# Two trunk layers on one core: earlier bank readers and splits in the first layer, half products by row blocks, a bank counted free a tick later, GpSimd's sum first

## The chip, the cores and the metric

The kernel runs on one core of one Trainium2 chip. The metric is the device time of one execution in microseconds (us), the median of the runs shown. Smaller is better.

## What is computed

Two post-norm layers over 512 rows of 1024 columns, in float32. Cut to what matters:

```python
def even_layer(x):                                  # layer 0
    q, k, v, g_ret, xb, g_lru = split(x @ w_in)     # each 1024 wide, 8 heads of 128
    ret = group_norm(retention(rope(q), rope(k), v)) * silu(g_ret)
    lru = rg_lru_branch(xb) * silu(g_lru)           # causal conv of width 4, two gate products, scan
    return concat(ret, lru) @ w_out

def odd_layer(x):                                   # layer 1
    q, k, v, g = split(x @ w_in)                    # 16 query/key heads of 128, 8 value heads of 256
    out = (softmax(q1 k1) - lam * softmax(q2 k2)) @ v     # causal, per head
    out = out * rsqrt(mean(out ** 2) + eps) * subln_g * (1 - lambda_init) * silu(g)
    return out @ w_out

for layer in (even_layer, odd_layer):
    x = layer_norm(alpha * x + layer(x))
```

## The kernel before

Every float32 product is three fp32r matmuls (`mm3`, L155): each operand is split into a high part, cast on ScalarE (L152), and a low part, the difference, on VectorE (L153). That holds for the weights as well, which come by DMA as 128x1024 pieces named w0, w1, ... in the order of use. There are five buffers of split weights, so a weight's cast has to wait until TensorE is done with the weight five places earlier (w89 takes the buffer of w84). A piece's DMA, cast and subtraction run ahead of its use as far as these buffers let them.

TensorE's order is written out by hand. The big projections form the backbone; after each of their steps (a *tick*, `side.tick()`) a queue, `Side`, may place one small step of retention, RG-LRU or attention, as soon as the number of ticks that its generator yielded has gone by (`RET_START`, `LRU_GATES`, `ATT_FREE` and the like). SyncE's DMA order is also written by hand. The orders of ScalarE, VectorE and GpSimd come out of a scheduler, by priorities: `tc.high_priority(n)` lifts what stands under it by n. Each engine then runs its list strictly from front to back.

Products leave TensorE in PSUM banks: four for the big ones (`pj`), two for scores and gates (`sc`), one for attention values (`av`) and one for transposes (`tp`). A product that takes a bank again waits for the last reader of what was in it.

Layer 0, RG-LRU (`lru`, one column block c of 128 at a time): ScalarE reads the product xb twice out of its bank, as a copy (L553) and scaled (L555, tile xc); three VectorE steps finish the convolution (L558); xc is split; after `LRU_GATES[c]` ticks TensorE multiplies it by the gate weights (pr, then pi). `silu` (L483, L484) reads the gate projections gl and gr. Retention (`rs`, rsd, r) and the output product out0 (columns of head 0 and 1) stand between these on TensorE.

Layer 1: the query and key projections of one head run while the attention of another is placed between them. For heads 2 to 7 the gate (g) and value (v) projections are not made as two products: `gates_values` (gv1, gv2, gv3) forms them from seven half products over block sums of the operands, prepared beforehand. `product` walks such a half product; its first two, into the banks gv?a0, gv?a1 and gv?b0, gv?b1, use the plain blocks of x. Attention of head hd and row block qb has these steps: scores as, masked maximum (L694), exponential e (L697), weights wt (transposed, split as w12, w13 and so on after the head and the block), values po, then GpSimd's mean of squares ave (L733) and power ars (L395), the normed block o on VectorE (L736), o's transposes back into po's bank, and the split of those into om, the operand of the output product oo. With one `av` bank the next po has to wait until om of the block before has been read.

```python
        if own:
            av[0] = side.now + ATT_FREE
```

This line (L744) tells the queue when the bank may be asked for again; `spare[0]` is true in the stages that make queries and keys.

The last layer norm: the output product of the last heads ends with row blocks 2 and 3. For block 2 (`late`), one half of the columns goes over ScalarE and GpSimd (L419, L420, L424), the other over VectorE; for block 3 both halves go over VectorE (L428, L430). `rsqrt` (L395) is GpSimd's power. Four output DMAs on SyncE close the kernel.

Of the kernel before, what the change touches and what calls it, by code (L numbers as in the profile page):

```python
# [11 lines left out]
ALU = mybir.AluOpType  # L12
# [5 lines left out]
KT = D // P  # L18
SB = S // P
# [8 lines left out]
RET_START = (13, 13, 13, 13, 13, 13, 13, 8)  # L28
RET_SCORES = (4, 4, 4, 7)
RET_NORM = (8, 7, 8, 7, 8, 6, 5, 5)  # L30
LRU_GATES = (12, 12, 13, 12, 12, 12, 9, 12)
LN_TURN = 15
ATT_START, ATT_GAP = (12,) * 7 + (7,), (8,) * 7 + (7,)
ATT_SCORES = (7, 7, 7, 8)
# [3 lines left out]
ATT_FREE, ATT_LENT = 2, 8  # L38

P_ROPE, P_SCORES, P_SQUARE, P_GROUP, P_VALUE = 50, 13, 60, 5, 60  # L40
P_CONV, P_GATES = 9, 5
P_LN, P_LAST, P_WEIGHTS, P_ATT = 10, 10, 450, 337
P_LAST_GROUP = 500
WARM_UP = 8
EARLY = 2

# [57 lines left out]
def trunk(ctx: ExitStack, tc: tile.TileContext, a):  # L104
# [289 lines left out]
    def rsqrt(var, out):  # L394
        nc.gpsimd.tensor_tensor(out=out, in0=var, in1=nhalf[:, :1], op=ALU.pow)  # L395

    def layer_norm(y, sb, gb, late=False, src=None, then=lambda: None):
        hv = [y[:, sb, hf * HALF:hf * HALF + HALF] for hf in range(2)]
        src = [hv[0], src or hv[1]]
        st = stats.pop(sb, None)  # L400
        if st is None:
            st = small.tile([P, 2, 6], F32, tag="bst", name="bst", bufs=2)
            for hf in range(2):
                nc.vector.bn_stats(out=st[:, hf], in_=hv[hf])
        mv = small.tile([P, 2], F32, tag="bmv", name="bmv", bufs=2)
        nc.vector.bn_aggr(out=mv, in_=st)
        rs = small.tile([P, 1], F32, tag="lrs", name="lrs", bufs=2)
        ve = small.tile([P, 1], F32, tag="rs", name="lve")
        nc.vector.tensor_scalar(out=ve, in0=mv[:, 1:2], scalar1=EPS, scalar2=None, op0=ALU.add)  # L409
        rsqrt(ve, rs)  # L410
        then()
        if late:


            nc.vector.scalar_tensor_tensor(out=hv[0], in0=hv[0], scalar=mv[:, 0:1], in1=gb[0][0], op0=ALU.subtract, op1=ALU.mult)
            yield
            nm = small.tile([P, 1], F32, tag="lnm", name="lnm", bufs=1)
            tc.keep_in_program_order(nc.vector.tensor_scalar(out=nm, in0=mv[:, 0:1], scalar1=rs, scalar2=-1.0, op0=ALU.mult, op1=ALU.mult))
            nc.scalar.activation(out=hv[1], in_=hv[1], func=AF.Identity, scale=rs, bias=nm)  # L419
            nc.gpsimd.tensor_tensor(out=hv[1], in0=hv[1], in1=gb[0][1], op=ALU.mult)  # L420
            yield
            tc.keep_in_program_order(nc.vector.scalar_tensor_tensor(out=hv[0], in0=hv[0], scalar=rs, in1=gb[1][0], op0=ALU.mult, op1=ALU.add))
            yield 0, hv[0]
            tc.keep_in_program_order(nc.gpsimd.tensor_tensor(out=hv[1], in0=hv[1], in1=gb[1][1], op=ALU.add))  # L424
            yield 1, hv[1]
            return
        for hf in range(2):
            nc.vector.scalar_tensor_tensor(out=hv[hf], in0=src[hf], scalar=mv[:, 0:1], in1=gb[0][hf], op0=ALU.subtract, op1=ALU.mult)  # L428
        for hf in range(2):
            nc.vector.scalar_tensor_tensor(out=hv[hf], in0=hv[hf], scalar=rs, in1=gb[1][hf], op0=ALU.mult, op1=ALU.add)  # L430
            yield hf, hv[hf]
# [116 lines left out]
            split(n1, cut(m, ALL, h % 2))  # L548

    def lru(c, ps, m):  # L550
        with tc.high_priority(P_CONV):
            xb = temp(f"xbp{c}")
            nc.scalar.copy(out=xb, in_=ps)  # L553
            xc = temp(f"xc{c}")
            nc.scalar.activation(out=xc, in_=ps, func=AF.Identity, scale=conv_w(3, c), bias=conv_b(c))  # L555
            for w in range(3):
                sh = 3 - w
                nc.vector.scalar_tensor_tensor(out=xc[:, sh:], in0=xb[:, :S - sh], scalar=conv_w(w, c), in1=xc[:, sh:], op0=ALU.mult, op1=ALU.add)  # L558
        with tc.high_priority(P_GATES):
# [12 lines left out]
        nc.scalar.activation(out=i, in_=pi, func=AF.Sigmoid, bias=gbx(c))  # L572

        nc.scalar.activation(out=t, in_=t, func=AF.Tanh, scale=sp4[:, c:c + 1])
        nc.vector.tensor_tensor(out=i, in0=i, in1=xc, op=ALU.mult)  # L575
        d = xc
        r = temp(f"r{c}")

        nc.scalar.activation(out=r, in_=t, func=AF.Ln, bias=1.0)
        nc.scalar.activation(out=r, in_=r, func=AF.Exp, scale=-1.0)  # L580
        nc.vector.scalar_tensor_tensor(out=d, in0=t, scalar=1.0, in1=r, op0=ALU.add, op1=ALU.mult)
        nc.vector.scalar_tensor_tensor(out=d, in0=d, scalar=2.0, in1=r, op0=ALU.subtract, op1=ALU.mult)  # L582
        nc.scalar.activation(out=r, in_=t, func=AF.Sqrt)  # L583
# [26 lines left out]
    for kind, i in ev:  # L610
        if kind == "v":
            if i:
                for j in range(4):
                    side.need(job["ret", j], lambda: j in seen)
            v = v_even(i)
        elif kind == "xb":
            if i % 2 == 0:
                raw = load(f"gw{i}", [P, 4 * P], a["gw"][i // 2], pl=es, tag="es")
                gw[0] = pair(two, [P, 4 * P], "gw", f"gw{i}", bufs=1)
                split(raw, gw[0])  # L620
            job["lru", i] = side.add(lru(i, t_unit(x, f"xb{i}"), mixes(("lru", i // 2))), "lru", 2)
        elif kind == "q":
            dec[i] = load(f"dec{i}", [P, S], a["dec"][i], pl=two, tag="dec")
            q[i] = rope(t_unit(x, f"q{i}"), "q", f"q{i}")
        elif kind == "k":
            job["ret", i] = side.add(retention(i, q.pop(i), rope(t_unit(x, f"k{i}"), "k", f"k{i}"), v, dec.pop(i), mixes(("ret", i // 2))), "ret", 1, RET_START[i])
        elif kind in ("ro", "lo", "out"):
            even_out({"ro": ("ret",), "lo": ("lru",), "out": ("lru", "ret")}[kind], i, f"{kind}{i}")
        else:
            ps = t_unit(x, f"{kind}{i}")  # L630
            if len(users) >= 5:
                side.need(job[users[-5]])
            users.append(("ret" if kind == "gr" else "lru", i))
            g = gp.tile([P, S], F32, tag="g", name=f"{kind}{i}")
            silu(ps, g, f"{kind}{i}")
            gates[kind, i] = g
        if (kind, i) == ("gr", 1):
            for sb in range(SB):
                nc.sync.dma_start(out=y[:, sb], in_=a["x"][sb])
# [44 lines left out]
    def attention(hd, qb, q, k, m):  # L684
# [57 lines left out]
            split(pm.rearrange("p (i s) -> p i s", s=P), cut(m, ALL, ALL, slice(qb * P, qb * P + P)))  # L742

        if own:  # L744
            av[0] = side.now + ATT_FREE

    oj, om, vs, vt, av = {}, {}, {}, {}, [0]

# [67 lines left out]
    def gates_values(i):  # L816
# [3 lines left out]
        def total(k):  # L820
            return lambda kt, n: tuple(sx[:, k, x, kt, n * P:n * P + P] for x in range(2))

        def product(ps, left, start, then=lambda: None):
            for j in range(2):
                if j:
                    then()
# [24 lines left out]
        one = [bank(ps_pj, "pj", f"gv{i}a{n}") for n in range(2)]  # L851
        two = [bank(ps_pj, "pj", f"gv{i}b{n}") for n in range(2)]
        p1, u, p7, low = [], [], [], []
        product(one, block(0, 0), True)
        copies(one, "p1", p1)
        product(two, block(0, 1), True)
        gate(two, p1, 0)
        product(one, total(0), False)
        copies(one, "u", u)
# [19 lines left out]

    def odd_end(sb):  # L880
        nonlocal rest
        last = sb == SB - 1
        norm = layer_norm(y, sb, gb1, sb == SB - 2, residual.get(1) if last else None, (lambda: rest()) if last else (lambda: None))

        def steps():
            for t in norm:
                if t is not None:
                    nc.sync.dma_start(out=a["out"][sb, :, t[0] * HALF:t[0] * HALF + HALF], in_=t[1])
                if sb == SB - 2:
                    yield  # L890

        if sb == SB - 2:
            it = steps()
            next(it)
            rest = lambda: next(it, None)
        else:
            for _ in steps():
                pass

    def past(g):  # L900
        if g >= 0:
# [160 lines left out]
```

## Time and profile before

| | |
|---|---|
| median of 3 runs | 919.15 us (918.99 to 919.6) |
| profiled execution | 919.45 us |
| its span | 917.7 us |
| TensorE busy | 905.8 us, 99% of the span |
| VectorE busy | 718.1 us, 78% |
| ScalarE busy | 517.6 us, 56% |
| GpSimd busy | 113.1 us, 12% |

The span is what the profiler saw between the first and the last instruction; the profiled execution's own time is 1.75 us longer. The engines are PE (TensorE), DVE (VectorE), ACT (ScalarE), POOL (GpSimd) and SP (SyncE). A row of a timeline gives an instruction's start in the span, how long it took, its line, what it wrote and read, and, in brackets, how long its engine was idle before it and whom it waited for. The end of a matmul is modelled, so the rows of TensorE overlap.

### The profile page before, as it was taken

What the parts mean: (1) busy time and instruction counts of PE and PEld (TensorE: products, weight loads), DVE (VectorE), ACT (ScalarE), POOL (GpSimd) and SP (SyncE); (2) the same over time, 40 slices, a digit from 0 to 9 for tenths busy, and PEclk for the clock granted to TensorE, in tenths of its full rate; (3) what the DMA queues carried; (4) which work ended last, traced back from release to release, by engine and by line L of the source; (5) the groups of instructions that cost most, each with busy time, mean ns of one, the idle gap of its engine ahead of it and who ended that gap; (6) DMA issues with size and microseconds to landing.
All of it is one profiled execution on the core that took longest, in us unless ns stands there. A gap on an engine that the chain in (4) does not pass through costs nothing.

```text
span 917.7 us, 11876 instructions
## 1 busy us (share of the span) xinstructions
PE 905.8 (99%) x4258; PEld 750.6 (82%) x4258; DVE 718.1 (78%) x1191; ACT 517.6 (56%) x846; POOL 113.1 (12%) x190
## 2 busy tenths in 40 slices
PE   9999999999999999999999999999999999999996
PEld 7888887888888888888888878888888888888885
DVE  5887977958868998897868887748877668867687
ACT  5567787546575668533456666435655355665440
POOL 2311010110102010010101120000120100201112
PEclk9999999999999999999999999999999999999999
DMA  8985463872829471434842226646247382178102
GB/s 288 283 278 149 125 186 91 245 203 58 263 78 270 113 205 51 169 129 149 326 179 70 69 70 229 229 161 252 70 136 250 142 321 92 58 265 276 45 1 92
DMA packets 46524, 152.93 MB, mean 167 GB/s; under 512 B 6145, under 2 KB 6273, under 8 KB 45697
## 3 DMA queue, kind: packets, MB, share of 16 engines
q1 hardware_dynamic: 41472, 135.39, 41.5%
q0 software_dynamic: 4992, 16.78, 9.5%
q8 instruction: 33, 0.54, 0.2%
q14 instruction: 27, 0.21, 0.1%
HBM read 139.57 MB, written 37.75 MB: 193 GB/s over the span
## 4 chain that ended last, share of the span: by engine, by line
PE 87%; DVE 6%; ACT 3%; issue 2%; POOL 1%; DMA 1%; SPq 0%; DVEq 0%; ACTq 0%; POOLq 0%
PE oo_ps L157 8%; PE gr_ps L157 5%; PE out_ps L157 4%; PE q_ps L157 4%; PE gl_ps L157 4%; PE ev_ps L157 4%; PE k_ps L157 4%; PE xb_ps L157 4%; PE po L157 3%; PE as L157 3%; PE ov_ps L157 2%; PE gv3a L157 2%; PE gv2a L157 2%; PE eo_ps L157 2%; PE og_ps L157 2%; PE gv3b L157 2%
## 5 line engine op out<-in xcount | busy, mean ns | idle before, releaser
L697 ACT ACTIVATE e<-as,nm 128x128 f32<-128x128 f32 (+3 forms) x64 | 33.2, 524 | 33.5 <-DVE nm L694 33.3
L704 POOL TENSOR_SCALAR zr<-z 128x1 f32<-128x1 f32 x32 | 16.4, 511 | 248.1 <-ACT e L697 248.1
L736 DVE SCALAR_TENSOR_TENSOR o<-po,ars,og 128x256 f32<-128x256 f32 x32 | 15.5, 484 | 35.0 <-POOL ars L395 35.0
L186 POOL DMA_DIRECT2D t<-t x24 | 19.2, 799 | 160.3 <-DMA t<-in_od_w 157.7
L733 POOL TENSOR_SCALAR ave<-ss,zr 128x1 f32<-128x1 f32 x32 | 16.4, 512 | 141.2 <-ACT po L730 135.2
L186 POOL DMA_DIRECT2D t<-in_od_w x24 | 19.1, 796 | 117.9 <-DMA t<-in_od_w 117.8
L694 DVE CUSTOM_DVE_ANT_0 as<-as,mask 128x128 f32<-128x128 f32 (+3 forms) x64 | 30.4, 506 | 2.3 <-PE as L157 2.3
L730 ACT ACTIVATE po<-po 128x256 f32<-128x256 f32 x32 | 11.9, 371 | 24.6 <-PE po L157 24.4
L575 DVE TENSOR_TENSOR xbp<-xbp,xc 128x512 f32<-128x512 f32 x8 | 5.5, 692 | 17.5 <-ACT xbp L572 17.5
L395 POOL TENSOR_TENSOR ars<-ave,nhalf 128x1 f32<-128x1 f32 x32 | 18.8, 587 | 2.7
L705 DVE SCALAR_TENSOR_TENSOR e<-e,zr,e 128x128 f32<-128x128 f32 (+3 forms) x32 | 17.6, 549 | 0.8
L558 DVE SCALAR_TENSOR_TENSOR xc<-xbp,vecs,xc 128x509 f32<-128x509 f32 (+2 forms) x24 | 17.8, 744 | 0.2
L395 POOL TENSOR_TENSOR lrs<-lve,nhalf 128x1 f32<-128x1 f32 x8 | 7.3, 912 | 83.1 <-DVE lve L409 83.1
L514 DVE TENSOR_TENSOR rsd<-rs,dec 128x512 f32<-128x512 f32 (+3 forms) x32 | 15.5, 484 | 2.1 <-PE rs L157 1.9
L278 DVE TENSOR_TENSOR y<-oo_ps,y 128x512 f32<-128x512 f32 x23 | 15.3, 685 | 2.2 <-PE oo_ps L157 2.1
L567 ACT ACTIVATE t<-pr,vecs 128x512 f32<-128x512 f32 x8 | 5.5, 688 | 17.5 <-PE pr L157 17.4
L709 PE MATMUL wt<-ident,e 128*128 128x128 f32 x80 | 13.9, 272 | 0.0
L152 ACT CAST hh<-ht 128x512 fp32r<-128x512 f32 x8 | 4.7, 588 | 15.5 <-PE ht L654 15.5
L709 PEld LDWEIGHTS wt<-ident,e 128*128 128x128 f32 x80 | 10.5, 140 | 3.4
L583 ACT ACT_TABLE_LOAD x8 | 10.3, 1283 | 4.2 <-DVE xc L582 4.1
L702 DVE RECIPROCAL zr<-z 128x1 f32<-128x1 f32 x32 | 5.2, 162 | 9.6 <-ACT e L697 9.4
L697 ACT ACTIVATION_READ_ACCUMULATOR e<-as,nm 128x1 f32 x64 | 12.5, 195 | 0.0
(2844 smaller groups left out, 3478.0 us busy)
## 6 DMA issues: line engine op xcount, KB each, us to landing
w_r<-in_od_w SPq DMA_DIRECT2D x58, 512.0 KB, 5.9
w_r<-in_ev_w SPq DMA_DIRECT2D x47, 512.0 KB, 5.1
t<-in_od_w SPq DMA_DIRECT2D x48, 256.0 KB, 5.5
sx<-sd SPq DMA_DIRECT2D x24, 512.0 KB, 5.7
w_r<-t SPq DMA_DIRECT2D x24, 512.0 KB, 3.3
w_r<-in_ev_wo SPq DMA_DIRECT2D x16, 512.0 KB, 4.5
w_r<-in_od_wo SPq DMA_DIRECT2D x16, 512.0 KB, 4.7
t<-in_od_w POOLq DMA_DIRECT2D x24, 256.0 KB, 5.2
```

The source lines that it names most:

```text
L157: nc.tensor.matmul(out=out, lhsT=l[n == 2], rhs=r[n == 1], start=start and n == 0, stop=stop and n == 2, **kw)
L186: nc.gpsimd.dma_start(out=dst, in_=two, max_dma_last_dim=4 * D, accum_op=ALU.add)
L395: nc.gpsimd.tensor_tensor(out=out, in0=var, in1=nhalf[:, :1], op=ALU.pow)
L514: nc.vector.tensor_tensor(out=s[:, :n], in0=ps[:, :n], in1=dec[:, :n], op=ALU.mult)
L558: nc.vector.scalar_tensor_tensor(out=xc[:, sh:], in0=xb[:, :S - sh], scalar=conv_w(w, c), in1=xc[:, sh:], op0=ALU.mult, op1=ALU.add)
L694: nc.vector.tensor_tensor_reduce(out=ps[:, :n], in0=ps[:, :n], in1=mask[:, S - n:], scale=-QK_SCALE, scalar=3.0e38, op0=ALU.add, op1=ALU.m ...
L697: nc.scalar.activation(out=e, in_=ps[:, :n], func=AF.Exp, scale=-1.0, bias=nm, accum_out=z[:, mp:mp + 1])
L704: nc.gpsimd.tensor_scalar(out=zr[:, 1:2], in0=z[:, 0:1], scalar1=z[:, 0:1], scalar2=EPS, op0=ALU.mult, op1=ALU.mult)
L705: nc.vector.scalar_tensor_tensor(out=ee[0], in0=ee[1], scalar=zr[:, 0:1], in1=ee[0], op0=ALU.mult, op1=ALU.add)
L709: nc.tensor.transpose(out=pt[:, kb * P:kb * P + P], in_=ee[0][:, kb * P:kb * P + P], identity=ident)
L733: nc.gpsimd.tensor_scalar(out=ve, in0=ss, scalar1=zr[:, 1:2], scalar2=None, op0=ALU.add)
L736: nc.vector.scalar_tensor_tensor(out=o, in0=po[:, :2 * P], scalar=rs, in1=gates[qb, hd // 2][:, hc:hc + 2 * P], op0=ALU.mult, op1=ALU.mult)
```

## The change

Five parts. In layer 0, the two ScalarE reads of xb's bank for columns 3 and 5, their split, and the silu of the gates gl3 and gl5 get priority 80 (before 9, 5 and 0), as does the split of xc7; the gate products of column 3 come one tick later. In `gates_values` the first two half products go by row blocks: both weights are taken at the start and all four steps of the first row block come ahead of those of the second. Outside the query and key stages the `av` bank is counted free one tick later. In the last layer norm GpSimd's add stands right behind its multiply, and the closures that issued the two are simpler.

```diff
-LRU_GATES = (12, 12, 13, 12, 12, 12, 9, 12)
+LRU_GATES = (12, 12, 13, 13, 12, 12, 9, 12)
...
+P_CONV, P_GATES, P_OUT = 9, 5, 80
+OUT_NEXT = (3, 5)
...
             nc.gpsimd.tensor_tensor(out=hv[1], in0=hv[1], in1=gb[0][1], op=ALU.mult)
+            nc.gpsimd.tensor_tensor(out=hv[1], in0=hv[1], in1=gb[1][1], op=ALU.add)
             yield
             tc.keep_in_program_order(nc.vector.scalar_tensor_tensor(out=hv[0], in0=hv[0], scalar=rs, in1=gb[1][0], op0=ALU.mult, op1=ALU.add))
-            yield 0, hv[0]
-            tc.keep_in_program_order(nc.gpsimd.tensor_tensor(out=hv[1], in0=hv[1], in1=gb[1][1], op=ALU.add))
-            yield 1, hv[1]
+            yield from enumerate(hv)
...
-        with tc.high_priority(P_CONV):
+        with tc.high_priority(P_OUT if c in OUT_NEXT else P_CONV):
             xb = temp(f"xbp{c}")
             nc.scalar.copy(out=xb, in_=ps)
             xc = temp(f"xc{c}")
             nc.scalar.activation(out=xc, in_=ps, func=AF.Identity, scale=conv_w(3, c), bias=conv_b(c))
...
-        with tc.high_priority(P_GATES):
+        with tc.high_priority(P_OUT if c in OUT_NEXT or c == 7 else P_GATES):
             t2 = part(S, f"xc{c}")
             split(xc, t2)
...
-            silu(ps, g, f"{kind}{i}")
+            with tc.high_priority(P_OUT if kind == "gl" and i in OUT_NEXT else 0):
+                silu(ps, g, f"{kind}{i}")
...
-            av[0] = side.now + ATT_FREE
+            av[0] = side.now + ATT_FREE + (not spare[0])
...
+            if apart:
+
+                ws = [take(3) for _ in range(2)]
+                for n in range(2):
+                    for kt in range(KT // 2):
+                        c = kt % 2 * HALF
+                        mm3(ps[n], left(kt, n), cut(ws[kt // 2], ALL, slice(c, c + HALF)), kt == 0, kt == KT // 2 - 1)
+                        side.tick()
+                return
...
-        product(one, block(0, 0), True)
+        product(one, block(0, 0), True, apart=True)
...
-        product(two, block(0, 1), True)
+        product(two, block(0, 1), True, apart=True)
```

Where this moves instructions is shown at three places. In all rows the number after a name counts tiles and has no other meaning; lines of the changed kernel lie one or two away.

ScalarE in layer 0, where out0 of the first head pair runs (xb3_ps is the bank that out0 takes next), before:

```order
L152 CAST w24h_1352<-w24_r_1351 128x1024
L152 CAST retm0h_639<-rq1_1168 128x512
L152 CAST w25h_1572<-w25_r_1571 128x1024
L152 CAST lrum1h_1036<-xc2_1063 128x512
L152 CAST r20h_1330<-rsd20_1328 128x512
L553 COPY xbp3_1379<-xb3_ps_1308 128x512
L555 ACTIVATE xc3_1381<-xb3_ps_1308,vecs_204 128x512
```

And after:

```order
L153 CAST w24h_1352<-w24_r_1351 128x1024
L153 CAST w25h_1572<-w25_r_1571 128x1024
L153 CAST lrum1h_1036<-xc2_1063 128x512
L553 COPY xbp3_1379<-xb3_ps_1308 128x512
L555 ACTIVATE xc3_1381<-xb3_ps_1308,vecs_204 128x512
L153 CAST retm0h_639<-rq1_1168 128x512
L153 CAST r20h_1330<-rsd20_1328 128x512
```

The two reads of xb3's bank, L553 and L555, now stand ahead of the casts of retm0 and r20. On VectorE, gl3 (L484) moves six rows forward in the same stretch, from behind the scan (L587) and rq1's last product (L547) to ahead of rq1's first (L542).

TensorE at the start of gv1, before:

```order
L157 MATMUL gv1a0_4926<-w84h_4751,hh_3481 128x512
L157 MATMUL gv1a0_4926<-w84l_4752,hh_3481 128x512
L157 MATMUL gv1a0_4926<-w84h_4751,hl_3482 128x512
L157 MATMUL gv1a1_4927<-w84h_4751,hh_3481 128x512
L157 MATMUL gv1a1_4927<-w84l_4752,hh_3481 128x512
L157 MATMUL gv1a1_4927<-w84h_4751,hl_3482 128x512
L157 MATMUL gv1a1_4927<-w84h_4751,hh_3481 128x512
L157 MATMUL gv1a1_4927<-w84l_4752,hh_3481 128x512
L157 MATMUL gv1a1_4927<-w84h_4751,hl_3482 128x512
L709 MATMUL wt12_4954<-ident_3479,e102_4872 128x128 x3
L157 MATMUL gv1a0_4926<-w85h_4837,hh_3481 128x512
```

And after:

```order
L158 MATMUL gv1a0_4926<-w84h_4751,hh_3481 128x512
L158 MATMUL gv1a0_4926<-w84l_4752,hh_3481 128x512
L158 MATMUL gv1a0_4926<-w84h_4751,hl_3482 128x512
L158 MATMUL gv1a0_4926<-w85h_4837,hh_3481 128x512
L158 MATMUL gv1a0_4926<-w85l_4838,hh_3481 128x512
L158 MATMUL gv1a0_4926<-w85h_4837,hl_3482 128x512
L158 MATMUL gv1a0_4926<-w85h_4837,hh_3481 128x512
L158 MATMUL gv1a0_4926<-w85l_4838,hh_3481 128x512
L158 MATMUL gv1a0_4926<-w85h_4837,hl_3482 128x512
L711 MATMUL wt12_4960<-ident_3479,e102_4872 128x128 x3
L158 MATMUL gv1a1_4927<-w84h_4751,hh_3481 128x512
```

The second row block (gv1a1) with w84 stood ahead of the first block's w85; now it comes behind it, and w84 is in use until later.

VectorE in gv1, from e103 (attention of head 1, map 0, block 3) to om1l of the block before, before:

```order
L705 SCALAR_TENSOR_TENSOR e103_4978<-e113_4986,zr_4988,e103_4978 128x512
L153 TENSOR_TENSOR w90l_5048<-w90_r_5046,w90h_5047 128x1024
L736 SCALAR_TENSOR_TENSOR o12_5035<-po12_5019,ars_5031,og02_4075 128x256
L153 TENSOR_TENSOR w91l_5108<-w91_r_5106,w91h_5107 128x1024
L694 ISA as200_5056,nm_5060<-as200_5056,mask_4095 128x128
L694 ISA nm_5060 128x1
L694 ISA as210_5064,nm_5068<-as210_5064,mask_4095 128x128
L694 ISA nm_5068 128x1
L847 TENSOR_TENSOR og10_5099<-gv1b0_4928,p110_5006 128x512
L702 RECIPROCAL zr_5072<-z_5055 128x1
L703 TENSOR_SCALAR zr_5072<-zr_5072,z_5055,nlam_3727 128x1
L153 TENSOR_TENSOR w13l_5086<-wt13_5080,w13h_5085 128x512
L705 SCALAR_TENSOR_TENSOR e200_5062<-e210_5070,zr_5072,e200_5062 128x128
L153 TENSOR_TENSOR om1l_4272<-po12_5019,om1h_4271 128x2x128
```

And after:

```order
L707 SCALAR_TENSOR_TENSOR e103_4978<-e113_4986,zr_4988,e103_4978 128x512
L154 TENSOR_TENSOR w89l_5012<-w89_r_5010,w89h_5011 128x1024
L738 SCALAR_TENSOR_TENSOR o12_5041<-po12_5025,ars_5037,og02_4075 128x256
L154 TENSOR_TENSOR w90l_5018<-w90_r_5016,w90h_5017 128x1024
L858 TENSOR_TENSOR og10_5099<-gv1b0_4928,p110_5006 128x512
L696 ISA as200_5056,nm_5060<-as200_5056,mask_4095 128x128
L696 ISA nm_5060 128x1
L696 ISA as210_5064,nm_5068<-as210_5064,mask_4095 128x128
L696 ISA nm_5068 128x1
L816 SCALAR_TENSOR_TENSOR og10_5099<-p110_5006,og10_5099 128x512
L704 RECIPROCAL zr_5072<-z_5055 128x1
L705 TENSOR_SCALAR zr_5072<-zr_5072,z_5055,nlam_3727 128x1
L707 SCALAR_TENSOR_TENSOR e200_5062<-e210_5070,zr_5072,e200_5062 128x128
L154 TENSOR_TENSOR w91l_5108<-w91_r_5106,w91h_5107 128x1024
L154 TENSOR_TENSOR w13l_5086<-wt13_5080,w13h_5085 128x512
L154 TENSOR_TENSOR om1l_4272<-po12_5025,om1h_4271 128x2x128
```

The split of w89, which before stood ten rows further up, comes here; w90l, w91l follow it one place later each, and L814 (L816 after) now stands ahead of om1l. gv2 and gv3 move alike: w115l and w141l come behind the row of e303 and e503, and w117l and w143l right ahead of om3l and om5l.

## Rows read from the trace of the kernel before

**Rows 1.** The page: the span, and busy time with share and instructions.

```profile
span 917.7 us, 11876 instructions
...
PE 905.8 (99%) x4258; PEld 750.6 (82%) x4258; DVE 718.1 (78%) x1191; ACT 517.6 (56%) x846; POOL 113.1 (12%) x190
```

**Rows 2.** Timeline of TensorE: start, duration, instruction, idle before it.

```profile
139.26 0.51 PE L157 MATMUL out_ps<-w21h,lrum0h 128*128 128x512 f32 x1 [0.37 <-DVE gl L484]
...
140.46 0.38 PE L157 MATMUL rs<-q2h,k2h 128*128 128x256 f32 x1 [0.23 <-DVE rsd L514]
...
142.28 0.50 PE L157 MATMUL out_ps<-w21h,lrum0h 128*128 128x512 f32 x1 [0.50 <-ACT xc L555]
...
342.76 0.50 PE L157 MATMUL pr<-xc7l,gw6h 128*128 128x512 f32 x1 [0.41 <-DVE xc7l L153]
...
533.47 0.39 PE L157 MATMUL gv1a<-w84h,hl 128*128 128x512 f32 x1
534.27 0.50 PE L157 MATMUL gv1a<-w84h,hh 128*128 128x512 f32 x1 [0.41 <-DVE om1l L153]
534.61 0.40 PE L157 MATMUL gv1a<-w84l,hh 128*128 128x512 f32 x1
...
543.31 0.51 PE L157 MATMUL gv1b<-w86h,hh 128*128 128x512 f32 x1 [0.20 <-DVE om1l L153]
...
551.35 0.39 PE L157 MATMUL po<-ov00h,w13h 128*128 128x256 f32 x1 [0.22 <-DVE om1l L153]
...
596.44 0.39 PE L157 MATMUL po<-ov10h,w22h 128*128 128x256 f32 x1 [0.16 <-DVE om2l L153]
```

**Rows 3.** Timeline of ScalarE and VectorE in out0 of layer 0.

```profile
134.14 0.60 ACT L483 ACTIVATE gl_sg<-gl_ps 128x512 f32<-128x512 f32 x1
...
138.53 0.68 DVE L484 TENSOR_TENSOR gl<-gl_ps,gl_sg 128x512 f32<-128x512 f32 x1
...
147.79 0.68 DVE L153 TENSOR_TENSOR xc3l<-xc,xc3h 128x512 fp32r<-128x512 f32 x1
```

**Rows 4.** Timeline of VectorE at the gate product of column 7.

```profile
342.03 0.68 DVE L153 TENSOR_TENSOR xc7l<-xc,xc7h 128x512 fp32r<-128x512 f32 x1
```

**Rows 5.** Timeline of VectorE in gv1.

```profile
538.53 1.22 DVE L153 TENSOR_TENSOR w89l<-w_r,w89h 128x1024 fp32r<-128x1024 f32 x1
...
544.64 1.23 DVE L153 TENSOR_TENSOR w90l<-w_r,w90h 128x1024 fp32r<-128x1024 f32 x1 [0.72 <-ACT w90h L152]
...
550.88 0.42 DVE L153 TENSOR_TENSOR om1l<-po,om1h 128x256 fp32r<-128x256 f32 x1
551.21 0.68 DVE L814 SCALAR_TENSOR_TENSOR og<-p,og 128x512 f32<-128x512 f32 x1
```

**Rows 6.** Timeline of GpSimd, VectorE and TensorE in gv2.

```profile
666.70 1.47 POOL L733 TENSOR_SCALAR ave<-ss,zr 128x1 f32<-128x1 f32 x1 [1.06 <-ACT po L730]
...
666.87 1.22 DVE L153 TENSOR_TENSOR w116l<-w_r,w116h 128x1024 fp32r<-128x1024 f32 x1
...
672.21 0.42 DVE L153 TENSOR_TENSOR om3l<-po,om3h 128x256 fp32r<-128x256 f32 x1
...
674.10 0.28 PE L157 MATMUL po<-ov10h,w33h 128*128 128x256 f32 x1
```

**Rows 7.** The page's groups: count, busy time, mean ns, idle before.

```profile
L733 POOL TENSOR_SCALAR ave<-ss,zr 128x1 f32<-128x1 f32 x32 | 16.4, 512 | 141.2 <-ACT po L730 135.2
...
L395 POOL TENSOR_TENSOR ars<-ave,nhalf 128x1 f32<-128x1 f32 x32 | 18.8, 587 | 2.7
```

**Rows 8.** Timeline of GpSimd and VectorE in the last 9 us.

```profile
909.35 1.45 POOL L420 TENSOR_TENSOR y<-y,ln 128x512 f32<-128x512 f32 x1 [1.25 <-ACT y L419]
911.20 0.92 POOL L395 TENSOR_TENSOR lrs<-lve,nhalf 128x1 f32<-128x1 f32 x1 [0.40 <-DVE lve L409]
912.09 1.26 POOL L424 TENSOR_TENSOR y<-y,ln 128x512 f32<-128x512 f32 x1
...
912.29 2.27 DVE L430 SCALAR_TENSOR_TENSOR y<-y,lrs,ln 128x512 f32<-128x512 f32 x2
```

More of the change, by code (lines that the diff above doesn't have):

```diff
@@ L40 @@
 P_ROPE, P_SCORES, P_SQUARE, P_GROUP, P_VALUE = 50, 13, 60, 5, 60
-P_CONV, P_GATES = 9, 5
+P_CONV, P_GATES, P_OUT = 9, 5, 80
 P_LN, P_LAST, P_WEIGHTS, P_ATT = 10, 10, 450, 337
 P_LAST_GROUP = 500
+OUT_NEXT = (3, 5)
 WARM_UP = 8
@@ L395, in rsqrt, with layer_norm @@
         nc.gpsimd.tensor_tensor(out=out, in0=var, in1=nhalf[:, :1], op=ALU.pow)
-    def layer_norm(y, sb, gb, late=False, src=None, then=lambda: None):
+    def layer_norm(y, sb, gb, late=False, src=None):
         hv = [y[:, sb, hf * HALF:hf * HALF + HALF] for hf in range(2)]
@@ L410, in layer_norm @@
         rsqrt(ve, rs)
-        then()
         if late:
@@ L555, in lru @@
             nc.scalar.activation(out=xc, in_=ps, func=AF.Identity, scale=conv_w(3, c), bias=conv_b(c))
+        with tc.high_priority(P_CONV):
             for w in range(3):
@@ L821, in total, with product @@
             return lambda kt, n: tuple(sx[:, k, x, kt, n * P:n * P + P] for x in range(2))
-        def product(ps, left, start, then=lambda: None):
+        def product(ps, left, start, then=lambda: None, apart=False):
+            if apart:
[6 more added lines that the diff above has]
+                return
             for j in range(2):
@@ L881, in odd_end @@
         nonlocal rest
-        last = sb == SB - 1
-        norm = layer_norm(y, sb, gb1, sb == SB - 2, residual.get(1) if last else None, (lambda: rest()) if last else (lambda: None))
+        norm = layer_norm(y, sb, gb1, sb == SB - 2, residual.get(1) if sb == SB - 1 else None)
         def steps():
             for t in norm:
-                if t is not None:
+                if t is None:
+                    yield
+                else:
                     nc.sync.dma_start(out=a["out"][sb, :, t[0] * HALF:t[0] * HALF + HALF], in_=t[1])
[L889 to L898, printed above, removed]
+        it = steps()
+        rest = lambda: next(it, None)
+        rest()
     def past(g):
```

## The prediction

> **What bounds the kernel now.** I read the page first: TensorE is busy 905.8 of 917.7 us [rows 1], and the chain that ended last lies on it almost throughout. So the kernel ends when TensorE has got through its hand-written list, and a change that leaves the list's length alone can win only what TensorE waits, plus the tail behind its last matmul. Next I read the waits of TensorE and looked each up in its timeline [rows 2]. The reader is to see there that idle time of TensorE understates a wait. gv1a at 534.27 shows 0.41 idle; its start lies 0.80 behind the row ahead, where neighbours lie 0.23 apart, and the next row follows after 0.34 instead of 0.23. So that wait costs 0.57 + 0.11 = 0.68: its idle figure plus about 0.28. With this the waits that the change aims at cost: gl in layer 0 0.65, rsd 0.51, xc 0.78, xc7l 0.69, gv1a 0.69, gv1b 0.48, the fourth attention block of head 1 (po at 551.35) 0.50, po at 596.44 0.44 and its twin one pair of heads later the same. That is 5.2 us, the most that can be won ahead of the tail.
>
> **The change, part by part.** Times below are of the profiled execution (919.45; span 917.7, 1.75 around it). I replayed the new order of each engine by hand: every instruction starts when its engine's predecessor and its inputs are done, and takes what the same instruction took in the trace.
>
> *Layer 0, out0.* VectorE's gl3 product now stands before rq1 instead of behind the scan. It ended 139.21, though its sigmoid was done by 134.74 [rows 3]. Its wait (0.65) goes. TensorE then reaches the rs product 0.65 earlier, but rsd comes only 0.38 earlier, being behind the rest of VectorE's queue: that wait grows by 0.27. ScalarE now reads xb3's bank ahead of retm0 and r20, so the wait for xc (0.78) goes too. Sum so far 0.65 - 0.27 + 0.78 = 1.16. What is late next is xc3l: it ended 148.47 [rows 3] and hardly moves (148.44 by the replay), as the three convolution steps and two weight splits stand ahead of it. TensorE, 1.16 earlier, and meeting the gate product one tick later than before, now waits about 0.6 for it where three short gaps summed to 0.17. Gain 1.16 + 0.17 - 0.6 = **0.73**; bounds 0.2 (xc3l as much later as one 128x512 subtraction) and 1.2 (no new wait). One more table load on ScalarE is covered: the normalised rq2 it precedes is needed microseconds later. The same raised priorities for column 5 leave every engine's order as it was: 0.
>
> *xc7.* xc7l is put ahead of q7l, one 128x512 subtraction of 0.6 net. It ended 342.71 [rows 4] and ends 342.1; TensorE is there at 342.19. The wait goes except for what is needed to start: **0.6** (0.4 to 0.69).
>
> *Half products by row blocks in gates_values.* TensorE's work is equal, and the waits gv1a and gv1b (0.69 + 0.48) go, since other matmuls now stand where the bank was late. But the first half product now keeps two split weights until its second row block is done; weight w89 uses w84's buffer, so its cast and its subtraction leave the place before w12l, where VectorE had time, and come behind e103. In gv1 VectorE's row of before is w89l at 538.53, w90l at 544.64, om1l ending 551.30 [rows 5]; of after: w89l (544.4 to 545.6), then o12 behind a wait for GpSimd, w90l, og, the maskings, L814's og, e200, w91l, w13l, om1l. Two instructions more than before stand between e103 and om1l: a weight split, 1.14 net of the overlap of 0.08, and L814's og, 0.60 net [rows 5]; the remaining 0.18 is waiting. The replay, with ScalarE's tanh ahead of the two exponentials and w91h behind them, gives om1l ending 553.22 instead of 551.30, so po starts at 553.27 instead of 551.35: **a loss of 1.92**, inside which the two waits removed are already swallowed, because TensorE would otherwise be there at 550.3 and now waits almost 3 us. Bounds: +1.3 (GpSimd 0.45 sooner and one overlap more) and +2.5 (tanh's og late by one 128x512 operation).
>
> gv2 and gv3 had no such wait: om3l ended 672.63 and po33 starts at 674.10 [rows 6], 1.4 to spare. Now w115l, which was split ahead of the block before, comes behind e303; w117l stands right ahead of om3l, and L814's og ahead of both. Replay: w115l to 667.4, w116l to 668.5, GpSimd's mean of squares and power to 669.2, o32 to 669.8, og, maskings, L814, e400 to 672.6, w33l, w117l to 674.5, om3l to 674.81. Against 674.10 - 0.04: a wait of 0.77 and 0.1 for the restart, **a loss of 0.87** in gv2 and, with identical order and the same distances, 0.87 in gv3. Bounds 0 and 1.3 each.
>
> The link that decides is GpSimd's mean of squares (L733): it takes 1.47 in gv2 and ends 0.08 behind w116l, the split beside it [rows 6], while the line's mean is 0.51 [rows 7]. If it starts ahead of w116l and takes 0.51, o32 is done 0.76 earlier, which all behind it follow, and gv2 and gv3 lose 0.1 each. [...]
>
> *The bank counted free a tick later.* In oo0 (po at 596.44) and its twin, one more product step stands ahead of the po products, and om2l ends 597.2 by the replay where TensorE is there at 597.9. Both waits go: **0.42 each**. In oo4 and oo6 there was no wait and none comes (0.25 us to spare at the closest).
>
> *The tail.* GpSimd's add ran 912.09 to 913.35 and made VectorE's first L430 take 1.6 of the 2.27 of two [rows 8]. Now the add follows its multiply at 910.80, ends near 912.06, and the power (0.92) ends 913.05 instead of 912.12. The two L430 then take 0.74 each: 914.5 instead of 914.56, and the last output is issued there. The add gives back what it takes: **0**, with -0.1 and +0.35 (if lve or L428 are held by the add) as bounds.
>
> Sum: -0.73 - 0.60 + 1.92 + 2 x 0.87 - 2 x 0.42 + 0 = **+1.49**. 919.45 + 1.49 = 920.94; the profiled execution stands 0.30 over the median of 919.15, so I forecast 920.6.
>
> **The rivals.**
> - *VectorE keeps up* (all waits go, none comes): it would be so if the late splits found a gap, for instance if ScalarE casts them earlier than its order and the replay let it. Then -0.73 - 0.6 - (0.69 + 0.48 + 0.5) - 0.84 = -3.8: 915.3. For it: VectorE is idle 0.72 ahead of w90l [rows 5]. Against: the order has w89l, w90l and w91l all ahead of om1l.
> - *GpSimd gets ahead of w116l*: +1.5 in gv1, 0.1 each in gv2 and gv3, with the other terms -0.5: 918.7.
> - *o late in all three stages*: the power behind o (L395) takes 0.92, as in the tail [rows 8], instead of its mean 0.59 [rows 7]. Nothing between o and om has room, so 0.33 to 0.4 goes 1:1 into each of three waits: +1.1 more, 921.8. It decides for slower from 0.12 per stage on, since my sum lies 0.35 under the bound below.
> - *Waits only move*: the reader behind each hastened one takes the gain, as rsd and xc3l do in out0, in xc7 and in oo as well (gains 0.2, 0.4 and 0), and the rows of gv cost as much in waits as before: 918.5. For it: that is what half of out0 does. Against: in oo0 nothing that TensorE needs next is as late as om2l was.
>
> **How the numbers follow.** A measurement of this kernel tells 0.2% (1.84 us) from no change. Forecast 0.48, own range 919.5 to 921.8, of which a third lies above 921.0; VectorE keeps up 0.17; GpSimd ahead 0.15; o late 0.13; waits only move 0.07. Faster than 917.3: 0.17. Slower than 921.0: 0.48/3 + 0.13, and a rest for the tail, 0.30. Same: 0.53. The range of 8 in 10 leaves out a tenth at each end: below 916.2 (more than half of the first rival) and above 922.6 (past o late and the upper bounds of gv).
>
> **What would show it.** In the changed kernel's profile: no TensorE wait on gl or xc in out0, but a longer one on rsd and a new one on xc3l near 148; none on xc7l; none at gv1a and gv1b, but one of 2 to 3 us at the po of head 1's fourth block, released by om1l, and one of about 0.6 idle at po33 and po53; none at the po of oo0 and oo2; L430 of two equal halves. I am wrong if the wait at that po is under 1 us (VectorE's queue was shorter than replayed), or if TensorE waits somewhere that I hold covered: w118 and later weights behind the late w117, or q30o behind the later om2.

## The result, and the profile after

The changed kernel takes 922.75 us (median of 6 runs, 922.3 to 925.28) against 919.53 us of the kernel before in the same comparison (6 runs, 918.99 to 920.04): a ratio of 1.0037, 95% interval 1.0027 to 1.0047. It is slower by 3.2 us. The forecast was 920.6, with no difference that can be told as the likeliest outcome, and its range ended at 922.6: the time lies 0.15 above it, where the forecast had put one chance in ten.

The waits of TensorE in the changed kernel (who waited on which line for whom: us in all, times, the longest):

```profile
PE po L158 <- DVE om1l L154: 3.1, 1, 3.1
...
PE po L158 <- DVE om5l L154: 0.6, 1, 0.6
PE po L158 <- DVE om3l L154: 0.6, 1, 0.6
PE rs L158 <- DVE rsd L513: 0.5, 1, 0.5
PE pr L158 <- DVE xc3l L154: 0.4, 1, 0.4
```

Against [rows 2]: the waits for gl, xc, xc7l, gv1a, gv1b, and the po of head 2 (with its twin in the next pair of heads) are gone. There stand instead the longer wait for rsd and the new one for xc3l in out0, and the three at po in gv1, gv2 and gv3 (3.1, 0.6 and 0.6 idle). These are the waits that the forecast named, at the places that it named. Its sum did not hold all the same, so the waits alone aren't the answer. The next view is the windows of gv1. After the stretch, its length and the busy times of PE, PEld, DVE, ACT and POOL, the third last number is the granted clock of TensorE:

```profile
548.00:551.00 3.00, 0.96 (x5) 0.46 (x3) 2.65 (x6) 3.00 (x9) 0.41 (x1) 1.00 0.00 0
551.00:553.00 2.00, 0.96 (x4) 0.96 (x5) 2.00 (x5) 0.89 (x2) 0.00 (x0) 0.62 0.00 0
553.00:554.00 1.00, 1.00 (x7) 1.00 (x6) 1.00 (x2) 0.25 (x1) 0.00 (x0) 0.50 0.00 0
554.00:555.00 1.00, 1.00 (x6) 1.00 (x6) 0.32 (x1) 0.00 (x0) 0.00 (x0) 0.55 0.00 0
555.00:556.00 1.00, 1.00 (x6) 0.78 (x6) 0.00 (x0) 0.74 (x3) 0.30 (x1) 1.00 0.00 0
```

TensorE stops at 549.0 and starts again at 552.0. In the stretches between 551 and 555 its granted clock is 0.62, 0.50 and 0.55, against 1.00 in those just ahead and behind. The five other executions were not traced, but the mean granted clock of each run is on record: 0.993 to 0.996 in the six of the changed kernel, 0.997 to 0.999 in all those of the kernel before that list it. The profiled one, at 0.996, is the fastest of the six, and the three at 0.993 are the three slowest (922.99, 923.09 and 925.28). By these figures the clock was down for a while in each of them, and in three for longer than this trace shows; where, no trace tells. TensorE's timeline shows what the lower clock does (start, duration, instruction, idle before):

```profile
548.57 0.39 PE L158 MATMUL gv1a<-w88h,sx 128*128 128x512 f32 x1
552.04 0.58 PE L158 MATMUL po<-ov00h,w13h 128*128 128x256 f32 x1 [3.08 <-DVE om1l L154]
552.42 0.41 PE L158 MATMUL po<-ov00l,w13h 128*128 128x256 f32 x1
...
554.55 0.41 PE L158 MATMUL po<-ov03h,w13l 128*128 128x256 f32 x1
554.77 0.46 PE L158 MATMUL gv1a<-w88h,sx 128*128 128x512 f32 x1
555.07 0.40 PE L158 MATMUL gv1a<-w88l,sx 128*128 128x512 f32 x1
```

The twelve matmuls of po lie (554.55 - 552.42) / 10 = 0.21 apart; in the trace of before the twelve of the same po are 0.12 apart, at a clock of 1.00. The wide ones from the row at 554.77 on are 0.30 and then 0.23 apart; in before the same ones are 0.23 apart.

To see where the time went I set each matmul's start in the one trace against the same matmul's in the other, at points where both lists are in step again, and took the difference from point to point:

| stretch | forecast | measured |
|---|---|---|
| the first 25 us, before anything changed | none | -0.52 |
| out0 of layer 0 | -0.73 | -0.66 |
| rs product of head 3 | none | +0.61 |
| gate product of column 7 | -0.60 | -0.61 |
| gv1 | +1.92 | +3.21 |
| oo0, oo2 | -0.42 each | -0.41, -0.43 |
| gv2, gv3 | +0.87 each | +0.87, +0.89 |
| last matmul to the end | 0 | -0.24 |
| the two spans (920.4 - 917.7) | +1.49 | +2.7 |

The first line is no effect of the change: the kernel before has a slow opening in its one trace, and all but one of the other traces of this study gain 0.1 to 0.9 on it there. What is left of the miss stands in two lines, gv1 and the rs product of head 3.

VectorE in gv1, of the changed kernel (L858 and L816 are L847 and L814 of [rows 5]):

```profile
543.15 1.22 DVE L154 TENSOR_TENSOR w89l<-w_r,w89h 128x1024 fp32r<-128x1024 f32 x1 [0.72 <-ACT w89h L153]
...
545.63 1.22 DVE L154 TENSOR_TENSOR w90l<-w_r,w90h 128x1024 fp32r<-128x1024 f32 x1
546.76 0.68 DVE L858 TENSOR_TENSOR og<-gv1b,p 128x512 f32<-128x512 f32 x1
...
548.20 0.69 DVE L816 SCALAR_TENSOR_TENSOR og<-p,og 128x512 f32<-128x512 f32 x1 [0.25 <-ACT p L815]
...
549.40 0.35 DVE L707 SCALAR_TENSOR_TENSOR e<-e,zr,e 128x128 f32<-128x128 f32 x1
549.83 1.22 DVE L154 TENSOR_TENSOR w91l<-w_r,w91h 128x1024 fp32r<-128x1024 f32 x1
550.97 0.68 DVE L154 TENSOR_TENSOR w13l<-wt,w13h 128x512 fp32r<-128x512 f32 x1
551.57 0.41 DVE L154 TENSOR_TENSOR om1l<-po,om1h 128x256 fp32r<-128x256 f32 x1
```

om1l ends 551.98, and po starts at 552.04. In TensorE's own time, which runs 1.22 ahead of before at that point, that is 1.9 later than in [rows 5]. The order and the times are those of the replay to 0.1.

The rs product of head 3, ScalarE's cast of w31 and TensorE:

```profile
178.24 1.05 ACT L153 CAST w31h<-w_r 128x1024 fp32r<-128x1024 f32 x1 [0.52 <-DMA w_r<-in_ev_w]
...
188.69 0.50 PE L158 MATMUL rs<-q3h,k3h 128*128 128x512 f32 x1
189.03 0.40 PE L158 MATMUL rs<-q3l,k3h 128*128 128x512 f32 x1
189.41 0.49 PE L158 MATMUL rs<-q3h,k3l 128*128 128x512 f32 x1
```

The rows lie 0.34 and 0.38 apart (the same three in before 0.24 and 0.23), with short waits ahead of the first and the third. The operands of k come just before them: k3h ends 188.64, k3l 189.36.

```profile
188.02 0.62 ACT L153 CAST k3h<-k_c 128x512 fp32r<-128x512 f32 x1 [4.63 <-DVE k_c L384]
188.67 0.69 DVE L154 TENSOR_TENSOR k3l<-k_c,k3h 128x512 fp32r<-128x512 f32 x1 [0.69 <-ACT k3h L153]
```

w31h waited for its DMA until 178.24; in the trace of before ScalarE was done with it at 176.39.

The tail, GpSimd and VectorE:

```profile
913.59 1.26 POOL L421 TENSOR_TENSOR y<-y,ln 128x512 f32<-128x512 f32 x1
914.81 1.00 POOL L396 TENSOR_TENSOR lrs<-lve,nhalf 128x1 f32<-128x1 f32 x1
...
913.90 1.50 DVE L427 SCALAR_TENSOR_TENSOR y<-y,bmv,ln 128x512 f32<-128x512 f32 x1
915.33 0.74 DVE L427 SCALAR_TENSOR_TENSOR y<-oo_ps,bmv,ln 128x512 f32<-128x512 f32 x1
915.99 1.40 DVE L429 SCALAR_TENSOR_TENSOR y<-y,lrs,ln 128x512 f32<-128x512 f32 x2
```

The add now holds VectorE's first L427 (1.50 us beside it, 0.74 for the second), not L429: the two L429 take 1.40 together, where the two L430 of before took 2.27 [rows 8].

GpSimd and VectorE in gv2:

```profile
668.91 1.22 DVE L154 TENSOR_TENSOR w116l<-w_r,w116h 128x1024 fp32r<-128x1024 f32 x1
...
669.00 1.29 POOL L735 TENSOR_SCALAR ave<-ss,zr 128x1 f32<-128x1 f32 x1 [2.79 <-DVE w115l L154]
```

### The profile page after: what moved, and what is told of

Same layout as the page of the kernel before. It is cut to its first block, busy times and chain, and to the rows that moved or that the text cites. A ratio compares the mean times of both kernels' runs of the same rounds, so it can differ in the third digit from the quotient of the medians.

```text
span 920.4 us, 11877 instructions
## 1 busy us (share of the span) xinstructions
PE 906.0 (98%) x4258; PEld 751.5 (82%) x4258; DVE 718.8 (78%) x1191; ACT 516.9 (56%) x847; POOL 107.9 (12%) x190
## 4 chain that ended last, share of the span: by engine, by line
PE 79%; DVE 9%; ACT 5%; issue 3%; POOL 2%; DMA 1%; SPq 0%; DVEq 0%; ACTq 0%; POOLq 0%
PE oo_ps L158 10%; PE q_ps L158 4%; PE gr_ps L158 4%; PE ev_ps L158 4%; PE xb_ps L158 4%; PE gl_ps L158 4%; PE k_ps L158 4%; PE out_ps L158 2%; PE po L158 2%; PE ov_ps L158 2%; PE eo_ps L158 2%; PE og_ps L158 2%; PE as L158 2%; PE gv3a L158 2%; PE gv2a L158 2%
## 5 line engine op out<-in xcount | busy, mean ns | idle before, releaser
L706 POOL TENSOR_SCALAR zr<-z 128x1 f32<-128x1 f32 x32 | 12.6, 395 | 247.5 <-ACT e L699 247.5
L742 PEld LDWEIGHTS po<-ident,o 128*128 128x128 f32 x64 | 8.9, 140 | 4.6 <-DVE o L738 0.5
```

## The experiments

All medians are against 919.06 to 919.08 us of the kernel before on the same chip (21 to 27 runs), except where another is named.

**Without the row blocks.**

```diff
-        product(one, block(0, 0), True, apart=True)
+        product(one, block(0, 0), True)
-        product(two, block(0, 1), True, apart=True)
+        product(two, block(0, 1), True)
```

Expected: 

> The change without its half products by row blocks (both in the old order); everything else of the change stays. Theory (the whole loss lies in the gv stages: VectorE's queue makes om late, TensorE waits there, and after the longest wait its clock is down): the waits of 3.1, 0.6 and 0.6 us are gone, the clock stays at 1.00 throughout, what is left is -0.7 in out0, +0.6 behind it at the rs product of head 3, -0.6 at column 7, -1.1 in oo0 and oo2: about 917.7, faster than before by 0.2%. Rival (the raised priorities of layer 0 or the later bank cost as much as they win, and the gv stages only part of the rest): 919.5 or more.

Measured: 917.22 us (10 runs), ratio 0.9978 (0.9969 to 0.9987). No wait is left at the po of gv1 beyond that of [rows 2], gv2 and gv3 have none, and against before gv1, gv2 and gv3 come to 0.0 each. So the row blocks make the whole loss, and the rest of the change is a gain of 1.8.

**The row blocks alone**, on the kernel before (the diff's part in `gates_values`, nothing else).

Expected: 

> The kernel before with nothing but the two half products by row blocks. Theory: the same three waits as in the changed kernel and the clock down after the first: +1.9 and +1.35 in gv1, +0.9 each in gv2 and gv3, together +5.0: about 924.5, slower than the whole change. Rival (the waits in gv come about only together with the gains in layer 0, which bring TensorE there earlier): the po wait in gv1 stays under 2 us, the clock at 1.00, and the time at 921 to 922.5.

Measured: 924.16 us (5 runs, 923.01 to 925.61), ratio 1.0057 (1.0044 to 1.0069). The waits are the same 3.1, 0.6 and 0.6. The execution that was profiled was the fastest of the five, and its windows in gv1 read:

```profile
551.00:553.00 2.00, 0.00 (x0) 0.00 (x0) 2.00 (x4) 1.53 (x3) 0.00 (x0) 1.00 0.00 0
553.00:554.00 1.00, 0.93 (x8) 0.93 (x9) 1.00 (x3) 0.36 (x1) 0.00 (x0) 1.00 0.00 0
```

The wait is as long as in the changed kernel, and the clock stayed at 1.00. There gv1 costs 1.96 instead of 3.21. So a wait of 3.1 us need not bring the clock down. Whether it did in the other four, which were not profiled, the record doesn't settle: their mean granted clocks are 0.996, 0.997, 0.998 and 0.995 at 924.07, 924.16, 924.39 and 925.61 us, against 0.998 in the profiled one. The slowest has the lowest clock, but two that are over 1 us slower than the profiled one have a clock as in the kernel before, so what made those slower stays open.

**The wait filled with work.**

```diff
+FILL = (1, 3, 4)
...
+        if (hd, qb) == FILL[:2]:
+            idle = bank(ps_sc, "sc", "idle13")
+            for _ in range(FILL[2]):
+                mm3(idle, cut(q[0], ALL, slice(0, P)), cut(k[0], ALL, ALL), True, True)
         for kb in range(qb + 1):
             mm3(po[:, :2 * P], ...
```

Expected: 

> The changed kernel with twelve extra matmuls of 128x512 (a score product of head 1 made four times into a bank that nobody reads) put right ahead of the po product that waits 3.1 us, so that TensorE works through most of that wait; nothing else moves on any engine. Theory (the clock, not the wait alone): the po product starts when it did, since om1l does not move, the granted clock stays at 1.00 from 548 to 556, its twelve matmuls lie 0.118 apart instead of 0.213, and the kernel is faster than the changed one by 1.3 or more: about 921.4. Rival (the slow matmuls behind the wait have another cause, or the extra work is simply added): as the changed kernel, 922.7, or up to 2.7 slower, 925.4.

Measured: 920.55 us (11 runs), ratio 1.0018 (1.0009 to 1.0027). The twelve matmuls are added work, and the kernel is 1.7 faster relative to before than the changed one (+1.49 against +3.22). Its windows where the changed kernel's clock was down:

```profile
551.00:553.00 2.00, 1.68 (x14) 1.63 (x14) 2.00 (x4) 0.63 (x1) 0.00 (x0) 1.00 0.00 0
553.00:554.00 1.00, 1.00 (x6) 0.82 (x5) 0.65 (x2) 0.69 (x3) 0.29 (x1) 1.00 0.00 0
```

The mean granted clock is 0.997 to 0.999 in all eleven executions. gv1 costs 1.96 here, as in the row blocks alone with the clock up, where the forecast had 1.92. Of what the two traces differ by, gv1 makes 1.25; the 0.61 at the rs product of head 3, which is 0.0 in this one, lies 360 us ahead of the fill, so the gain of 1.7 is not the clock's alone. That +1.49 is the forecast's sum to the hundredth is in part luck: in this trace 0.3 that was not forecast is lost behind gv3, and the tail is 0.24 shorter.

**Only the first half product by row blocks.**

```diff
-        product(two, block(0, 1), True, apart=True)
+        product(two, block(0, 1), True)
```

Expected: 

> The change with only the first half product (gv a) by row blocks, the second (gv b) in the old order. Theory (two things stand ahead of om in the changed kernel, and each comes from one of the half products: the late weight split from the first, the gate's second VectorE operation from the second): VectorE's order has w89l late but the gate's operation behind om1l, so om1l of gv1 ends about 1.1 later than before, not 1.9; TensorE waits 1.5 to 2.2 at that po; in gv2 and gv3 om3l comes 1.1 later, within the 1.4 to spare: no wait. 918.9 with the clock at 1.00, 920.2 with the clock down there. Rival (the late weight alone makes the loss): waits as in the whole change, 922.7.

Measured: 917.7 us (11 runs), ratio 0.9986 (0.9977 to 0.9995). TensorE's waits in gv1:

```profile
PE po L158 <- DVE om1l L154: 1.3, 1, 1.3
...
PE gv1b L158 <- DVE om1l L154: 0.7, 1, 0.7
```

The wait at gv1a is gone, that at gv1b is 0.7 instead of 0.2. om1l, and po behind it, come 0.91 later than before in TensorE's time, a little less than the 1.1 of one weight split; gv2 and gv3 lose nothing. The total was expected 1.2 too high: the wait was 1.3 and not 1.5 to 2.2, and the clock stayed.

**Only the second half product by row blocks** (the other line of the same diff).

Expected: 

> The change with only the second half product (gv b) by row blocks, the first (gv a) in the old order: the counterpart of the run with only the first. Theory (each half product puts one thing ahead of om): w89 is split early as before, but the gate's second VectorE operation and w91l stand ahead of om1l. om1l of gv1 ends about 0.7 later than before, the wait at gv1a stays (0.4 idle), that at gv1b goes, and the po behind waits 1.2 to 1.6; in gv2 and gv3 om3l comes about 1.1 later, within what is to spare. 0.7 over the change without row blocks (917.2): 917.9, clock at 1.00. Rival (the gate's operation finds room, as ScalarE and VectorE have idle time there): no wait over 0.6 at that po, 916.7.

Measured: 920.22 us (11 runs), ratio 1.001 (1.0002 to 1.0019). Both theories missed. om1l is as late as in the whole change, though w89 is split early. ScalarE, VectorE and TensorE in gv1:

```profile
546.80 0.63 ACT L815 ACTIVATE p<-og 128x512 f32<-128x512 f32 x1 [2.89 <-DVE og L858]
...
547.46 0.69 DVE L816 SCALAR_TENSOR_TENSOR og<-p,og 128x512 f32<-128x512 f32 x1 [0.49 <-ACT p L815]
...
548.95 0.16 DVE L704 RECIPROCAL zr<-z 128x1 f32<-128x1 f32 x1 [0.52 <-ACT e L699]
...
551.62 0.41 DVE L154 TENSOR_TENSOR om1l<-po,om1h 128x256 fp32r<-128x256 f32 x1
...
552.09 0.39 PE L158 MATMUL po<-ov00h,w13h 128*128 128x256 f32 x1 [2.57 <-DVE om1l L154]
```

ScalarE waits 2.89 for VectorE's og, VectorE 0.49 for the tanh and then 0.52 for the exponentials, which now stand behind the tanh on ScalarE. VectorE idles 1.0 there, where the whole change has one weight split more (1.14). The two causes don't add up: in gv1 the second half product alone makes 1.81 of lateness, the first alone 0.91, both 1.9. In gv2 they make 0.39, 0 and 0.87. Behind the wait of 2.57 the clock went down too. It was still at 1.00 when po began at 552.09, and fell about a microsecond later:

```profile
552.00:553.00 1.00, 0.91 (x7) 0.91 (x8) 1.00 (x3) 0.33 (x1) 0.00 (x0) 1.00 0.00 0
553.00:554.00 1.00, 1.00 (x8) 1.00 (x7) 1.00 (x2) 0.30 (x1) 0.00 (x0) 0.65 0.00 0
554.00:555.00 1.00, 1.00 (x4) 0.81 (x3) 0.37 (x1) 0.47 (x2) 0.27 (x1) 0.50 0.00 0
```

The eleven executions of this one kernel fall into two groups by their mean granted clock: the five at 0.997 to 0.999 took 918.84 to 920.11 us, the six at 0.995 and 0.996 (the profiled one, 921.43, among them) 920.22 to 921.72. The means of the groups lie 1.3 apart, about what the changed kernel's gv1 cost beyond its wait.

**The later free bank alone.**

```diff
-            av[0] = side.now + ATT_FREE
+            av[0] = side.now + ATT_FREE + (not spare[0])
```

Expected: 

> The kernel before with nothing but the av bank counted free one tick later outside the query and key stages. Theory: the waits at po22 and po42 go and nothing comes for them: -0.5 each, 918.0 against 919.06. Rival (what follows the later po is late in turn): 919.0.

Measured: 918.14 us (11 runs), ratio 0.999 (0.9981 to 0.9998). oo0 gives 0.44 and oo2 0.43, everything else behind the opening 0.

**The part in layer 0 alone** (priorities and `LRU_GATES`, on the kernel before).

Expected: 

> The kernel before with nothing but the raised priorities in layer 0 (with the gate products of column 3 one tick later). Theory: -0.7 in out0 and -0.6 at column 7; behind out0 the weight splits w26 to w31 run later than before, so that w31 comes late by DMA and k3l with it, and TensorE waits 0 to 0.6 at head 3's rs product, differing between executions: 918.0 (917.7 to 918.4). Rival (that wait is chance alone, and also stands in executions of the kernel before): 917.7 with no wait at rs of head 3 in its profile.

Measured: 918.02 us (11 runs, 917.71 to 920.31), ratio 0.9992 (0.9983 to 1.0001), so the gain is at the edge of what the runs can tell. Its trace is of the slowest of the eleven, with an opening 1.3 longer than in the trace of before. In it out0 gives -0.65, the rs product of head 3 +0.45, column 7 -0.55. The +0.45 goes with the part, by one trace of each kernel: those without it show 0.0 there (the kernel before, and the row blocks, the bank and the add, each alone), and those that have it 0 to 0.78, five of eight above 0.

**The convolution raised as well**, on the kernel without row blocks.

```diff
-        with tc.high_priority(P_CONV):
+        with tc.high_priority(P_OUT if c == 3 else P_CONV):
             for w in range(3):
```

Expected: 

> The change without row blocks (917.2), and with the three convolution steps of column 3 at the high priority as well, which brings xc3l six rows forward on VectorE. Theory (xc3l is the last thing late in out0): the new wait for xc3l (0.4 idle, 0.6 in all) goes, while rsd23 and r23l, which now stand behind xc3l, are needed later than it: 916.6. Rival (the place of xc3l is taken by the next reader, rsd or r23l, or by the out0 banks read later): 917.2 or more.

Measured: 915.97 us (5 runs, 915.61 to 916.19), ratio 0.9966 (0.9954 to 0.9979): faster than the kernel before by 3.1 and, by the two ratios, than the changed one by some 6.5. The longest waits of TensorE left in it:

```profile
PE idle L342 <- DVE epsb L336: 1.0, 1, 1.0
PE rs L158 <- DVE rsd L513: 0.6, 1, 0.6
PE gv1a L158 <- DVE om1l L154: 0.4, 1, 0.4
```

out0 gives -1.21 instead of -0.66, and the rs product of head 3 0.0. The theory held for xc3l, whose wait is gone; the gain, by the medians, is twice the 0.6 that it expected.

**The add alone**, on the kernel before (the diff's part in `layer_norm` and `odd_end`).

Expected: 

> The kernel before with nothing but GpSimd's add right behind its multiply in the last layer norm. Theory (the add only changes places: it holds VectorE's L428 instead of L430, and puts the power off by as much as L430 gains): from the end of the last matmul to the end of the last VectorE instruction 4.6 us instead of 4.67, time 919.0 against 919.07. Rival (the held L428 and the later power add up): 0.35 slower, 919.4, with the last L430 ending 5.0 behind the last matmul.

Measured: 919.03 us (11 runs), ratio 1.0 (0.9991 to 1.0008). VectorE's first L427, beside which the add runs from 910.42 to 911.68, takes 1.71, the second 0.74:

```profile
910.52 1.71 DVE L427 SCALAR_TENSOR_TENSOR y<-y,bmv,ln 128x512 f32<-128x512 f32 x1
```

From the end of the last matmul to the end of VectorE's last instruction it is 4.78, between the theory's 4.6 and the rival's 5.0; the time is the theory's.

**The score blocks raised too**, on the fastest kernel.

```diff
-            with tc.high_priority(P_SCORES if jb < SB - 1 else P_SQUARE):
+            with tc.high_priority(P_OUT if h == 2 and jb < 2 else P_SCORES if jb < SB - 1 else P_SQUARE):
```

Expected: 

> The fastest kernel so far (the change without row blocks, convolution of column 3 raised; 915.97), and with the first two score blocks of retention head 2 (rsd20, rsd21) at the high priority as well, which brings them three rows forward on VectorE. Theory (TensorE's one wait left in out0, 0.6 idle for rsd, is a matter of VectorE's order): that wait goes or falls under 0.2, and the time to 915.3. Rival (VectorE's list is full there, so that rq1's product and retm0 come later and TensorE waits for retm0l or xc3l in its place): 916.0 or more.

Measured: 917.66 us (11 runs), ratio 0.9985 (0.9976 to 0.9994). The wait for rsd goes, and two longer ones come:

```profile
PE out_ps L158 <- DVE w24l L154: 1.2, 1, 1.2
PE idle L342 <- DVE epsb L336: 1.0, 1, 1.0
PE out_ps L158 <- ACT xc L555: 0.7, 1, 0.7
```

The rival held, though not with the readers that it named: xc and w24l were pushed back.

## Why the prediction was wrong

*Layer 0.* Right in out0 (-0.66 for -0.73), with the moved wait for rsd and the new one for xc3l; the raised convolution then removed that for xc3l. Right at column 7 (-0.61 for -0.60). Wrong behind out0: "One more table load on ScalarE is covered" (a load takes 1.28 us in both traces) and with it all that follows out0 was costed at nothing. The later order of the splits w26 to w31 isn't covered; it costs 0 to 0.78, differing between executions. This wait stands only in traces of kernels with the part in layer 0. That TensorE waits there for k3h and k3l is in the rows above; that these are late by way of w31's later DMA is argued, and not shown: in the trace of the filled wait w31h also waits for its DMA (0.64) and nothing is lost.

*gv1.* This is the step that failed: "a loss of 1.92". The delay itself came out at 1.96 wherever the whole reordering ran with the clock up, so the lateness of om1l was right. What the step left out is what a wait of TensorE can cost beyond its own time, here 1.25 (3.21 less 1.96). The prediction itself said that TensorE "now waits almost 3 us" there, and priced those 3 us as a delay alone. In the changed kernel the clock was at 0.62, 0.50 and 0.55 in the windows of the twelve matmuls behind the wait, and gv1 cost 3.21; with the wait filled the clock stayed at 1.00 and gv1 cost 1.96. The windows of the row blocks alone stay at 1.00 behind a wait as long, so its length alone does not decide; what does, no run shows. The prediction listed no such rival, and its upper bound of 922.6 came from mechanisms that didn't occur: the rival "o late" did not come (the power took 0.57 in gv1 as before).

The working of the 1.92 was right in its sum. Its parts, 1.14 for the late weight and 0.60 for L814's og, describe VectorE's list when both stand in it; they are not what each half product costs, since the two apart showed 0.91 and 1.81, which overlap.

*gv2 and gv3.* Right: 0.87 and 0.89. The link named as the one that decides, GpSimd's mean of squares behind w116l, went as the replay had it: it started 0.09 behind w116l, took 1.29 against the line's mean of 0.51 [rows 7] and ended 0.16 behind it, and the rival that had GpSimd ahead fell. That a start ahead of w116l would bring the 0.51 was the author's estimate, and no run shows it: in [rows 6] the instruction starts 0.17 ahead of w116l, takes 1.47 all the same and ends 0.08 behind it. The two rows show it long beside the split in either order of the starts.

*The later bank.* Right: 0.41 and 0.43 for 0.42 each. *The tail.* Right for the add alone (no difference); it holds L427, the case for which the prediction's upper bound stood, and gives the time back at L429. In the changed kernel the tail was 0.24 shorter, past the lower bound of -0.1, as in every trace that has the later bank and the add together (0.21 to 0.24): L427 was held 1.50 there instead of 1.71. The prediction costed the two apart.

Of the 1.7 between the forecast's 1.49 and the measured 3.2, the clock is 1.25 (3.21 less 1.96) and the wait at head 3 0.6, less 0.2 at the end, by the changed kernel's one trace. That trace is of the fastest of the six executions; what the lower clock cost the three at 0.993 is not in it.

## What to carry to other kernels

Price a wait of the bounding engine twice: the time, and what the engine does after it; the waits of 0.6 us in gv2 and gv3 cost 0.87 to 0.91 each wherever they stood, the one of 3.1 us 1.96 or 3.21. When a change takes waits off one engine by a new order, look for what that order makes late on the others: here two waits worth 1.2 went, and om1l came 1.9 later. A replay of each engine's list with the durations of the trace places such waits to 0.1 us, but only where the replay was done: the stretch behind it, counted as covered, wasn't.

## What was unexpected of the hardware

TensorE's granted clock fell during a wait of 3.1 us (the changed kernel: 0.62 from 551 to 553, where a fall to 0.50 only when po starts at 552.04 would give 0.76) and about a microsecond after a wait of 2.6 had ended (only the second half product by row blocks: 1.00 in the window from 552, 0.65 in that from 553), and stayed at 1.00 through another wait of 3.1 us (the row blocks alone) and one of 1.3. The slow stretch behind it lasted from the first matmul to 554.77, 2.7 us, in the changed kernel. By the mean clocks of the other executions, the same kernel can meet it in some and not in others: six of eleven with only the second half product by row blocks, at 1.3 us more on the mean.
